# First norm and projections of a two-layer trunk: squares, scaling, partial sums and the values' first copy in another order

## The chip, the cores and the metric

The kernel runs on one NeuronCore of one Trainium2 chip. The core has five engines with an instruction queue each: TensorE (PE in the profile; its weight loads are PEld), VectorE (DVE), ScalarE (ACT), GpSimd (POOL) and SyncE (SP), which issues the transfers from memory. An engine runs its queue in order and waits, at the head of the queue, on semaphores that other engines or transfers raise. The metric is device microseconds (us) of one execution; lower is better.

## The reference

`x` is one sequence of 1024 tokens by 1024 features, `c` one vector of 1024 features. There are two layers. Layer 0 mixes tokens with softmax attention that has a forget gate (16 heads of 64), layer 1 with gated linear attention (4 heads); each is followed by a SwiGLU of 2816 hidden features. What matters here is the start of layer 0:

```python
mod = silu(c) @ ada_w[0] + ada_b[0]            # six vectors of 1024
sh1, sc1, g1, sh2, sc2, g2 = split(mod, 6)
h = rms_norm(x, norm1_g[0]) * (1 + sc1) + sh1   # norm: mean of squares over the 1024 features of a token
q, k, v, f_logit = split(h @ fox_w_in[0])       # 1024 + 1024 + 1024 + 16 columns
log_f = log_sigmoid(f_logit + b_f)
cum = cumsum(log_f, axis=tokens)
logits = q @ k.T / 8 + cum[t] - cum[s]          # causal, then softmax, times v, times fox_w_out
```

All is float32. Products are made from pairs: a tensor is split into a high part (rounded to the matmul's format fp32r) and a low part (the rest), and a product takes three matmuls, high by high, high by low, low by high.

## The kernel before

The start of the kernel (up to about 105 us) computes `h`, transposed (features on partitions), and with it, block by block, the first projections. It goes through these steps.

**Loads.** SP loads token tiles `xt[0..7]` of 128 tokens by 1024 features, the columns of `ada_w` for `sh1` and `sc1` in four pieces `d2 = 0..3` (piece `d2` gives the two vectors on the 256 features of blocks 2·d2 and 2·d2+1; tiles `adas`, two `k` of 128 rows in each), and the weights of the forget gate (`fw`), of the first two query heads (`wq0`) and key heads (`wk0`).

**Norm.** `sq_tile(t)` squares a token tile and sums over the features into `ssx` (ACT with an accumulator, L490, or DVE, L488). `ss_root(hf)` makes `1/sqrt` of four tiles' sums (DVE L494, POOL L495). `scale_tile` multiplies a tile by it in place (even tiles on DVE, L500; tiles 1 and 5 on ACT, L502; tiles 3 and 7 on POOL, L504).

**Modulation vectors.** For a piece `d2`, eight row blocks `k` are multiplied by `silu(c)` and added up. `ada0_pe` lets PE do some row blocks as matmuls with one moving column (L517, tile `mp`), `ada0_dve` lets DVE accumulate the others into `acc` (L527 the first, L529 the next ones), and `ada0_sum` adds `acc` over the partitions with four one-column matmuls (L535) and makes the two columns that `h_mod` needs (L538, L381). A one-column float32 matmul shows as two records in the profile.

**Blocks.** A block is (d, hf): feature block d of 128, token half hf of 512. `h_tr` transposes four token tiles into one PSUM bank (PE L551, tile `xp`, one bank for all blocks), `h_mod` applies the vectors (ACT L556 to `y`, ACT L558 the high part `h0h`, DVE for even d or POOL for odd d L559 the low part `h0l`), `first_k` runs the eight matmuls of the block for gate, query and key (PE L570 to L576): five need `h0h`, the last three need `h0l`. On PE a block's transposes are issued ahead of the previous block's eight matmuls.

**After the blocks.** `first_z(hf, acc)` makes the gate's logits (ACT L250, DVE L251, ACT L859, DVE L860) and, at the second half, log-sigmoid and the running sum over tokens: ACT Exp and Ln (L862, L863, each with a table load), DVE L864, the scan L865, and the transfers of the sum out and back (L866, L881). `q_evac` and `k_evac` copy the first queries and keys out of PSUM. `v_half` projects values for four heads: four token pairs `tp`, 48 matmuls each into one of two PSUM banks in turn (`vps`, L268 to L270), and `v_split` copies each pair out in two steps of ACT (L174) and DVE (L175). Then the attention loop begins; its first matmul is at L1006.

The order of the instructions of each engine from `begin` to the end of `v_half` is the order in which the program writes them: `in_order` chains them. Behind that, a planner with its own estimates places instructions.

Of the kernel before, what the change touches and what calls it, by code (L numbers as in the profile page):

```python
# [9 lines left out]
F32 = mybir.dt.float32  # L10
# [6 lines left out]
P = 128  # L17
# [36 lines left out]
def trunk(ctx, tc, x, c, ada_w, ada_b, norm1_g, norm2_g, ffn_w_in, ffn_w_out,  # L54
# [448 lines left out]
        else:  # L503
            nc.gpsimd.tensor_scalar(xs_, xs_, r, 1.0, op0=ALU.mult, op1=ALU.mult)  # L504

    NPE = (4, 0, 0, 0)
    modp = {}

    def ada0_pe(d2):

        mp = mp0([P, 2, 2], F32, f"mp{d2}")
        modp[d2] = (mp, acc2())
        n = 0
        for k in range(NPE[d2]):
            for j in range(2):
                for i in range(2):
                    nc.tensor.matmul(mp[:, j, i:i + 1], araw[(d2, k // 2)][:, k % 2, j, psl(i)], cact[:, k:k + 1],  # L517
                                     start=n == 0, stop=False)
                    n += 1

    def ada0_dve(d2, *ks):

        acc = modp[d2][1]
        for k in ks:
            a = araw[(d2, k // 2)][:, k % 2]
            if k == NPE[d2]:
                nc.vector.tensor_scalar(acc, a, cact[:, k:k + 1], None, op0=ALU.mult)  # L527
            else:
                nc.vector.scalar_tensor_tensor(acc, a, cact[:, k:k + 1], acc, op0=ALU.mult, op1=ALU.add)  # L529

    def ada0_sum(d2):
        mp, acc = modp.pop(d2)
        for j in range(2):
            for i in range(2):
                nc.tensor.matmul(mp[:, j, i:i + 1], acc[:, j, psl(i)], ones,  # L535
                                 start=NPE[d2] == 0 and j == i == 0, stop=j == 1 and i == 1)
# [318 lines left out]
    def first_z(hf, acc):  # L855
        cs = hsl(hf)
        f = zt[:, cs]
        sum16(f, ze[:, cs], acc[0][1])
        nc.scalar.activation(ze[:, cs], f, AF.Abs, bias=bf)  # L859
        nc.vector.tensor_scalar(zt[:, cs], f, bf, 0.0, op0=ALU.add, op1=ALU.min)  # L860
        if hf:
            nc.scalar.activation(ze, ze, AF.Exp, scale=-1.0)  # L862
            nc.scalar.activation(ze, ze, AF.Ln, bias=1.0)  # L863
            nc.vector.tensor_sub(zt, zt, ze)  # L864
            nc.vector.tensor_tensor_scan(cum, zt, zt, 0.0, ALU.add, ALU.bypass)  # L865
            nc.sync.dma_start(cum_d, cum)  # L866
            load_cum(0)
            load_cum(1)

    def v_split(g, tp, ps):  # L870
        v = vring([P, 2, 4, 2, 64], FR, f"v{g}{tp}")
# [21 lines left out]
    ada0_sum(0)  # L893
    wf_()
    wq0_()
    ada0_pe(1)
    ada0_dve(1, 0)
    wk0_()
    load_ada0(2)
# [4 lines left out]
    h_mod(0, 0)  # L904
    ada0_dve(1, 1, 2, 3)
    h_block(1, 0)
    ada0_dve(1, 4, 5, 6, 7)
    first_k(0, 0, accs[0])
    first_k(1, 0, accs[0])
    sq_tile(4)  # L910
    h_tr(2, 0)
    ada0_sum(1)
    sq_tile(5, True)
    h_mod(2, 0)
    h_block(3, 0)
    sq_tile(6, True)
    sq_tile(7)
    first_k(2, 0, accs[0])
    first_k(3, 0, accs[0])
    ada0_pe(2)  # L920
    ada0_dve(2, 0, 1)
    ss_root(1)
    for cs in (slice(0, HALF), slice(HALF, D)):
        for t in range(4, 8):
            scale_tile(t, cs)
    h_block(0, 1)
    ada0_dve(2, 2, 3, 4, 5, 6, 7)
    rest0 = [(0, 1), (1, 1), (2, 1), (3, 1), (4, 0), (5, 0), (4, 1), (6, 0), (7, 0), (5, 1), (6, 1), (7, 1)]
    done = []
    for n, (d, hf) in enumerate(rest0):  # L930
        if n:
            h_tr(d, hf)
        if n == 4:
            ada0_sum(2)
            ada0_pe(3)
            ada0_dve(3, 0, 1)
        if n == 7:
            ada0_sum(3)
        if n:
            h_mod(d, hf)  # L940
        if n in (4, 5, 6):
            ada0_dve(3, 2 * n - 6, 2 * n - 5)
        if n == 8:
            feed.depth = 1
            wvs[0] = [feed.next()]
        if n == 10:
            wvs[0].append(feed.next())
            first_z(0, accs[0])
        if n == 11:
            q_evac(accs[0][1][1], qkt[0], 0)  # L950
        if n:
            first_k(*rest0[n - 1], accs[rest0[n - 1][1]])
    k_evac(accs[0][2][1], qkt[0], 0)
    first_k(*rest0[-1], accs[1])
    first_z(1, accs[1])

    def v_half(g, half):

        if g not in vts:
            vts[g] = []  # L960
        if g not in wvs:
            wvs[g] = [feed.next(), feed.next()]
        for tp in range(2 * half, 2 * half + 2):
            ps = pj([P, 2, 256], F32, f"vps{g}{tp}")
            for i in range(2):
                yield from proj_tok(ps[:, i, :], wvs[g], hT, 2 * tp + i)
            v_split(g, tp, ps)
        if g or half:
            del wvs[g]

# [125 lines left out]
    acc0 = acc_r([P, 2, HALF], F32, "acc0")[:, 0, 0:256]  # L1096
    for j in (2, 3, 4, 5):
        ada0.q.append(ada_steps(0, j, acc0, wr, 4, 0))
    run(v_half(0, 0))
    q_evac(accs[1][1][1], qkt[0], 1)  # L1100
    k_evac(accs[1][2][1], qkt[0], 1)
    split_after.update((e, last_of(e)) for e in "ADG")
# [884 lines left out]
```

## Time and profile before

| | us |
|---|---|
| median of three runs (2415.0 to 2418.0) | 2417.4 |
| the profiled execution's own time | 2420.17 |
| its span | 2418.5 |
| PE busy in the span | 2369.3 |
| DVE, ACT, POOL busy | 1769.9, 1132.9, 1023.5 |
| start of the first value matmul (L268) | 79.10 |
| start of the first attention matmul (L1006) | 104.46 |

The profile is of one execution. A row of the timeline has its start, its length, engine, line, operation and tile, and in brackets how long the engine had stood idle before it and what ended that. Lengths of neighbouring matmuls overlap, so their speed is read from the distance of their starts. The table of stages gives the busy time of each engine, the clock granted to PE (1.00 is full) and the transfers' share.

### The profile page before, as it was taken

The page shows a single profiled execution, that of the slowest core. Times are in us where ns is not written, and L with a number is a line of the kernel's source. Part 1 is how long each engine was busy: PE and PEld are TensorE (multiplying, and loading weights), DVE is VectorE, ACT ScalarE, POOL GpSimd, SP SyncE. Part 2 cuts the span into 40 slices and gives each one's busy share as a digit, 9 for nine tenths or more (in the row PEclk, how much of TensorE's full clock was granted, in tenths as well). Part 3 has the DMA queues.
Part 4 walks back from the last instruction along what each step waited for, and adds up shares of the span by engine and source line. Part 5 has one row for each costly group of instructions (what it writes and reads, how often), then busy time and mean ns, then how long its engine had stood idle before and what let it go on. Part 6 is the DMA issues. An engine that isn't in the chain of part 4 may idle for free.

```text
span 2418.5 us, 35795 instructions
## 1 busy us (share of the span) xinstructions
PE 2369.3 (98%) x12328; PEld 2014.2 (83%) x12328; DVE 1769.9 (73%) x3020; ACT 1132.9 (47%) x2183; POOL 1023.5 (42%) x920
## 2 busy tenths in 40 slices
PE   6999999999999999999999999999999999999998
PEld 5888888878888888888888898888888888888888
DVE  6477878876688888876788676666587767666787
ACT  4665565666543333345324555454343334345325
POOL 3333333333335656653363222122335656653362
PEclk9999999999999999999999999999999999999999
DMA  8223423323326545457665243334325434347664
GB/s 254 63 88 96 129 82 121 115 96 114 122 90 194 178 161 173 163 184 260 226 211 170 59 127 95 114 117 167 109 92 179 157 132 156 130 169 257 230 211 148
DMA packets 340766, 359.24 MB, mean 149 GB/s; under 512 B 24220, under 2 KB 285496, under 8 KB 340584
## 3 DMA queue, kind: packets, MB, share of 16 engines
q1 hardware_dynamic: 340584, 356.95, 44.9%
q8 instruction: 97, 1.59, 0.3%
q14 instruction: 85, 0.70, 0.1%
HBM read 268.19 MB, written 88.67 MB: 148 GB/s over the span
## 4 chain that ended last, share of the span: by engine, by line
PE 85%; DVE 6%; DMA 3%; ACT 2%; issue 2%; SPq 1%; POOL 0%; DVEq 0%; POOLq 0%; ACTq 0%
PE p_b L268 16%; PE p_b L269 16%; PE p_b L270 16%; PE t_b L1038 2%; PE o_b L1052 2%; PE qk_b L268 2%; PE qk_b L269 2%; PE qk_b L270 2%; DMA ad_s<-in_ada_w_dram 1%; PE s_b L1006 1%; PE s_b L1007 1%; SPq L399 1%; PE vps_b L268 1%; PE vps_b L270 1%; PE vps_b L269 1%
## 5 line engine op out<-in xcount | busy, mean ns | idle before, releaser
L174 ACT CAST o_s<-xv_s 128x512 fp32r<-128x512 f32 (+1 forms) x376 | 217.7, 587 | 317.9 <-PE p_b L270 260.9
L175 DVE TENSOR_TENSOR o_s<-xv_s,o_s 128x512 fp32r<-128x512 f32 (+1 forms) x376 | 320.0, 854 | 59.6 <-ACT o_s L174 59.1
L269 PE MATMUL p_b<-B,o_s 128*128 128x512 f32 x608 | 237.6, 391 | 0.0
L270 PE MATMUL p_b<-B,o_s 128*128 128x512 f32 x608 | 237.0, 390 | 0.0
L268 PE MATMUL p_b<-B,o_s 128*128 128x512 f32 x608 | 236.3, 391 | 0.0
L1018 POOL TENSOR_SCALAR lp_s<-lp_s,st 128x128 f32<-128x128 f32 (+7 forms) x128 | 98.9, 777 | 288.3 <-DVE st L1017 257.5
L762 POOL TENSOR_TENSOR ex_s<-xv_s,xv_s 128x512 f32<-128x512 f32 (+1 forms) x64 | 87.7, 1371 | 271.2 <-DMA xv_s<-in_ffn_w_in_dram 107.0
L268 PE MATMUL p_b<-T,o_s 128*128 128x512 f32 x480 | 186.7, 389 | 0.0
L269 PE MATMUL p_b<-T,o_s 128*128 128x512 f32 x480 | 186.7, 389 | 0.0
L270 PE MATMUL p_b<-T,o_s 128*128 128x512 f32 x480 | 181.1, 389 | 0.0
L270 PEld LDWEIGHTS p_b<-B,o_s 128*128 128x128 f32 x608 | 114.7, 189 | 23.9
L269 PEld LDWEIGHTS p_b<-B,o_s 128*128 128x128 f32 x608 | 114.7, 189 | 23.7
L268 PEld LDWEIGHTS p_b<-B,o_s 128*128 128x128 f32 x608 | 114.7, 189 | 23.7
L1016 ACT ACTIVATE lp_s<-lp_s,st 128x128 f32<-128x128 f32 (+7 forms) x128 | 99.3, 777 | 71.4 <-DVE st L1012 69.1
L764 POOL TENSOR_TENSOR xv_s<-ex_s,xv_s 128x512 f32<-128x512 f32 (+1 forms) x64 | 84.9, 1326 | 68.8 <-DVE o_s L175 66.6
L174 ACT CAST pt_s<-t_b 128x512 fp32r<-128x512 f32 (+1 forms) x160 | 80.1, 547 | 69.1 <-PE t_b L1038 68.0
L1397 DVE TENSOR_TENSOR ex_s<-ex_s,p_b 128x512 f32<-128x512 f32 x140 | 93.7, 681 | 24.0 <-PE p_b L270 23.9
L227 POOL TENSOR_TENSOR w_l_s<-w__s,w_h_s 128x256 fp32r<-128x256 f32 x90 | 70.3, 810 | 93.9 <-ACT w_h_s L223 62.1
L175 DVE TENSOR_TENSOR pt_s<-t_b,pt_s 128x512 fp32r<-128x512 f32 (+1 forms) x160 | 96.4, 631 | 13.0 <-ACT pt_s L174 12.5
L268 PEld LDWEIGHTS p_b<-T,o_s 128*128 128x128 f32 x480 | 90.1, 188 | 18.7
L269 PEld LDWEIGHTS p_b<-T,o_s 128*128 128x128 f32 x480 | 90.1, 188 | 18.7
L270 PEld LDWEIGHTS p_b<-T,o_s 128*128 128x128 f32 x480 | 90.1, 188 | 18.6
(1937 smaller groups left out, 7404.6 us busy)
## 6 DMA issues: line engine op xcount, KB each, us to landing
xv_s<-in_ffn_w_in_dram SPq DMA_DIRECT2D x176, 256.0 KB, 3.2
hid_B<-x SPq DMA_DIRECT2D x70, 512.0 KB, 2.6
ad_s<-in_ada_w_dram SPq DMA_DIRECT2D x384, 64.0 KB, 2.4
hid_T<-x SPq DMA_DIRECT2D x36, 512.0 KB, 2.8
xv_s<-in_ffn_w_out_dram SPq DMA_DIRECT2D x96, 192.0 KB, 5.0
ada_s<-in_ada_w_dram SPq DMA_DIRECT2D x128, 128.0 KB, 2.9
xv_s<-in_ffn_w_out_dram SPq DMA_DIRECT2D x40, 256.0 KB, 2.9
T2o<-hid_T SPq DMA_DIRECT2D x18, 512.0 KB, 8.4
```

What stands on the lines that cost most here:

```text
L174: nc.scalar.copy(hi, src)
L175: nc.vector.tensor_sub(lo, src, hi.bitcast(F32))
L227: (nc.gpsimd if i < 3 else nc.vector).tensor_sub(lo[:, cs], rw[:, cs], hi[:, cs].bitcast(F32))
L268: nc.tensor.matmul(ps, ah, bh, start=start, stop=False)
L269: nc.tensor.matmul(ps, ah, bl, start=False, stop=False)
L270: nc.tensor.matmul(ps, al, bh, start=False, stop=stop)
L762: nc.gpsimd.tensor_add(s1, a21, a22)
L764: nc.gpsimd.tensor_sub(a11, s1, a11)
L1016: nc.scalar.activation(lp, lp, AF.Exp, bias=mcur, scale=-1.0, accum_out=st[:, qi, 2:3])
L1018: nc.gpsimd.tensor_scalar(lp, lp, st[:, qi, 3:4], 1.0, op0=ALU.mult, op1=ALU.mult)
L1038: nc.tensor.transpose(tp[:, i, :], lps[qi][:, psl(2 * b + jj)], ident)
L1397: nc.vector.tensor_add(d, d if src is None else dest(G, src), ps)
```

## The change

Seven edits, all in the steps above; the arithmetic is the same.

- Piece 1's row blocks 6 and 7 go from DVE to PE: `ada0_pe(1)` now issues eight one-column matmuls (sixteen records), behind the matmuls of block (1, 0).
- The squares of tiles 5 and 6 go from DVE to ACT, that of tile 7 from ACT to DVE. `ss_root(1)` is issued ahead of block (3, 0).
- The second token half's scaling is issued in two parts: features 0 to 511 ahead of block (0, 1), features 512 to 1023 (`slice(HALF, D)`) in block (4, 0)'s turn, behind two accumulation steps of piece 3.
- Piece 2's accumulation is spread differently, piece 3's starts two turns sooner, and its sum (`ada0_sum(3)`) is made a turn later, since block (5, 1) now stands ahead of (6, 0) and (7, 0).
- The value weights are split in turns 6 and 8 in place of 8 and 10.
- The first gate half (`first_z(0)`) is issued in turn 11, and the queries' copy behind the turns: both now behind the last block's `h_mod`.
- `gates_end` takes Ln, subtraction, scan and the sum's transfers out of `first_z`; `v_half` calls it behind the copy of its first token pair.

The order of SP's transfers stays the same. Far behind, at the start of layer 1 (near 1330 us), the planner also places a few instructions differently: the four matmuls that spread the norm (L601) stand nine value matmuls sooner, a value copy (ACT, DVE), a gate copy on ACT and two gate matmuls are shifted by one or two places.

```diff
-    NPE = (4, 0, 0, 0)
-    modp = {}
+
+    PE_K = (range(0, 4), range(6, 8), (), ())
+    accs0, mps0 = {}, {}
...
-        for k in range(NPE[d2]):
+        for k in PE_K[d2]:
...
         if hf:
             nc.scalar.activation(ze, ze, AF.Exp, scale=-1.0)
-            nc.scalar.activation(ze, ze, AF.Ln, bias=1.0)
-            nc.vector.tensor_sub(zt, zt, ze)
-            nc.vector.tensor_tensor_scan(cum, zt, zt, 0.0, ALU.add, ALU.bypass)
-            nc.sync.dma_start(cum_d, cum)
-            load_cum(0)
-            load_cum(1)
+
+    def gates_end():
+        nc.scalar.activation(ze, ze, AF.Ln, bias=1.0)
+        nc.vector.tensor_sub(zt, zt, ze)
+        nc.vector.tensor_tensor_scan(cum, zt, zt, 0.0, ALU.add, ALU.bypass)
+        nc.sync.dma_start(cum_d, cum)
+        load_cum(0)
+        load_cum(1)
...
-    ada0_pe(1)
     ada0_dve(1, 0)
...
     h_block(1, 0)
-    ada0_dve(1, 4, 5, 6, 7)
+    ada0_dve(1, 4, 5)
     first_k(0, 0, accs[0])
     first_k(1, 0, accs[0])
+    ada0_pe(1)
     sq_tile(4)
     h_tr(2, 0)
     ada0_sum(1)
-    sq_tile(5, True)
+    sq_tile(5)
+    sq_tile(6)
+    sq_tile(7, True)
     h_mod(2, 0)
+    ss_root(1)
     h_block(3, 0)
-    sq_tile(6, True)
-    sq_tile(7)
+    ada0_dve(2, 0)
     first_k(2, 0, accs[0])
     first_k(3, 0, accs[0])
-    ada0_pe(2)
-    ada0_dve(2, 0, 1)
-    ss_root(1)
-    for cs in (slice(0, HALF), slice(HALF, D)):
-        for t in range(4, 8):
-            scale_tile(t, cs)
+    for t in range(4, 8):
+        scale_tile(t, slice(0, HALF))
+    ada0_dve(2, 1, 2)
     h_block(0, 1)
-    ada0_dve(2, 2, 3, 4, 5, 6, 7)
-    rest0 = [(0, 1), (1, 1), (2, 1), (3, 1), (4, 0), (5, 0), (4, 1), (6, 0), (7, 0), (5, 1), (6, 1), (7, 1)]
-    done = []
+    ada0_dve(2, 3, 4, 5, 6, 7)
+    rest0 = [(0, 1), (1, 1), (2, 1), (3, 1), (4, 0), (5, 0), (4, 1), (5, 1), (6, 0), (7, 0), (6, 1), (7, 1)]
+
+    steps = {2: (0, 1), 4: (2, 3), 5: (4, 5), 6: (6, 7)}
     for n, (d, hf) in enumerate(rest0):
         if n:
             h_tr(d, hf)
         if n == 4:
             ada0_sum(2)
-            ada0_pe(3)
-            ada0_dve(3, 0, 1)
-        if n == 7:
+        if n == 8:
             ada0_sum(3)
         if n:
             h_mod(d, hf)
-        if n in (4, 5, 6):
-            ada0_dve(3, 2 * n - 6, 2 * n - 5)
-        if n == 8:
+        ada0_dve(3, *steps.get(n, ()))
+        if n == 4:
+            for t in range(4, 8):
+                scale_tile(t, slice(HALF, D))
+        if n == 6:
             feed.depth = 1
             wvs[0] = [feed.next()]
-        if n == 10:
+        if n == 8:
             wvs[0].append(feed.next())
+        if n == 11:
             first_z(0, accs[0])
-        if n == 11:
-            q_evac(accs[0][1][1], qkt[0], 0)
         if n:
             first_k(*rest0[n - 1], accs[rest0[n - 1][1]])
+    q_evac(accs[0][1][1], qkt[0], 0)
     k_evac(accs[0][2][1], qkt[0], 0)
...
-    def v_half(g, half):
+    def v_half(g, half, then=None):
...
             v_split(g, tp, ps)
+            if then is not None and tp % 2 == 0:
+                then()
...
-    run(v_half(0, 0))
+    run(v_half(0, 0, gates_end))
```

More of the change, by code (lines that the diff above doesn't have):

```diff
@@ L504, in scale_tile @@
             nc.gpsimd.tensor_scalar(xs_, xs_, r, 1.0, op0=ALU.mult, op1=ALU.mult)
-    NPE = (4, 0, 0, 0)
-    modp = {}
+    PE_K = (range(0, 4), range(6, 8), (), ())
+    accs0, mps0 = {}, {}
     def ada0_pe(d2):
-        mp = mp0([P, 2, 2], F32, f"mp{d2}")
-        modp[d2] = (mp, acc2())
+        mp = mps0[d2] = mp0([P, 2, 2], F32, f"mp{d2}")
         n = 0
-        for k in range(NPE[d2]):
+        for k in PE_K[d2]:
             for j in range(2):
@@ L521, in ada0_dve @@
     def ada0_dve(d2, *ks):
-        acc = modp[d2][1]
         for k in ks:
             a = araw[(d2, k // 2)][:, k % 2]
-            if k == NPE[d2]:
+            if d2 not in accs0:
+                acc = accs0[d2] = acc2()
                 nc.vector.tensor_scalar(acc, a, cact[:, k:k + 1], None, op0=ALU.mult)
             else:
+                acc = accs0[d2]
                 nc.vector.scalar_tensor_tensor(acc, a, cact[:, k:k + 1], acc, op0=ALU.mult, op1=ALU.add)
     def ada0_sum(d2):
-        mp, acc = modp.pop(d2)
+        if d2 not in mps0:
+            ada0_pe(d2)
+        mp, acc = mps0.pop(d2), accs0[d2]
         for j in range(2):
@@ L535, in ada0_sum @@
                 nc.tensor.matmul(mp[:, j, i:i + 1], acc[:, j, psl(i)], ones,
-                                 start=NPE[d2] == 0 and j == i == 0, stop=j == 1 and i == 1)
+                                 start=not PE_K[d2] and j == i == 0, stop=j == 1 and i == 1)
         ds_ = slice(2 * d2, 2 * d2 + 2)
```

## The prediction, made before the changed kernel had run

> **What bounds the kernel now.** The page's first part has PE busy for 98% of the span, so a gain must be PE time that is idle or slow. The table of stages shows where: up to 100 us PE is at 7 to 9 of 10, behind that at 10. I read PE's timeline there, its waits, then the engines that ended them.
>
> ```profile
> PE 2369.3 (98%) x12328; PEld 2014.2 (83%) x12328; DVE 1769.9 (73%) x3020; ACT 1132.9 (47%) x2183; POOL 1023.5 (42%) x920
> ```
> ```profile
> 30.00:40.00 10.00, 6.84 (x28) 5.40 (x28) 7.36 (x13) 3.94 (x6) 2.20 (x2) 0.83 1.08 353
> 60.00:70.00 10.00, 8.77 (x39) 7.37 (x40) 2.73 (x6) 5.04 (x8) 2.19 (x3) 0.83 0.01 2
> ```
> ```profile
> 31.84 1.05 PE L535 MATMUL mp_b<-ones,acc_s 128*128 128x1 f32 x8 [1.84 <-DVE acc_s L529]
> 34.22 0.80 PE L551 MATMUL xp_b<-ident,xt_s 128*128 128x128 f32 x4 [1.32 <-ACT y_s L556]
> 36.31 0.63 PE L572 MATMUL ks_b<-h0h,wk0h_s 128*128 128x512 f32 x1
> 36.74 0.63 PE L573 MATMUL ks_b<-h0h,wk0l_s 128*128 128x512 f32 x1
> 38.49 0.40 PE L572 MATMUL qs_b<-h0h,wq0h_s 128*128 128x512 f32 x1
> 38.72 0.39 PE L573 MATMUL qs_b<-h0h,wq0l_s 128*128 128x512 f32 x1
> ...
> 50.31 0.50 PE L574 MATMUL fs_b<-h0l,fw_s 128*128 128x512 f32 x1 [0.82 <-DVE h0l L559]
> 61.23 1.28 PE L535 MATMUL mp_b<-ones,acc_s 128*128 128x1 f32 x8 [1.75 <-DVE acc_s L529]
> 72.66 0.50 PE L574 MATMUL fs_b<-h0l,fw_s 128*128 128x512 f32 x1 [0.67 <-POOL h0l L559]
> 76.92 0.50 PE L570 MATMUL fs_b<-h0h,fw_s 128*128 128x512 f32 x1 [1.01 <-ACT h0h L558]
> ```
> ```profile
> 92.88 0.36 PE L268 MATMUL vps_b<-wv_0h_s,h0h 128*128 128x256 f32 x1 [2.13 <-DVE v_s L175]
> ```
>
> The brackets, with 0.46, 0.28 and 0.87 us more between 40 and 43, add up to 11.2 us of idle PE from 29 us on. PE also falls to half speed twice: starts of 512-column matmuls lie 0.43 us apart at 36.31 and 0.23 at 38.49. The clock of 0.83 in two stages says 1.7 us lost in each. So about 14.5 us are there to be won, 0.6% of the time.
>
> Two more rows set what DVE and POOL can do side by side:
>
> ```profile
> 36.60 1.53 DVE L527 TENSOR_SCALAR acc_s<-adas_s,cact 128x512 f32<-128x512 f32 x1
> ```
> ```profile
> 36.56 1.28 POOL L559 TENSOR_TENSOR h0l<-y_s,h0h 128x512 fp32r<-128x512 f32 x1 [9.26 <-ACT h0h L558]
> ```
>
> The same L527 takes 0.48 us alone (52.82). Here it ends 0.29 us behind POOL's instruction: a DVE instruction that starts under a POOL subtraction is held until that ends.
>
> **The change part by part,** placed on each engine in its new order, with lengths from this trace.
>
> *Piece 1's sum.* DVE loses two accumulation steps of 0.76 us: `acc` is ready at 30.2 in place of 31.8. PE gains sixteen one-column records behind 29.40. L535's records are 0.10 us apart when PE is at speed (51.6) and 0.21 when not (L517, 28 in 6.1 us): 1.6 or 3.4 us. PE had just run 512-column matmuls 0.23 apart, so I take 1.6. Transposes (0.4) follow, the sum from 31.5 (0.8), the columns (0.45), and `y` of (2, 0) starts at 32.8, not 33.38. With 3.4 us and slow transposes it starts near 35.4, and this stage ends 2.3 us later than I say.
>
> *Squares.* ACT does tiles 4, 5, 6 (1.2 us each with the accumulator's read). SP's rows that reuse a tile's semaphore put the landings of 5, 6, 7 at 29.7, 31.0, 32.3, so ACT is done at 32.3, ahead of `y`: the two added squares are hidden by the wait for piece 1, with 0.5 us to spare; a piece 1 that came sooner would gain nothing. DVE does tile 7 from 32.75 to 34.0 (1.3). Queued behind it are `h0l` of (2, 0), which PE needs only at 36.4, and L494, at 35.1. POOL's root (1.03) now stands ahead of `h0l` of (3, 0), which is then ready at 37.7; PE wants it at 38.9. Scaled halves are ready at 38.5. Before, squares, root and scaling ended at 41.5 and PE stood waiting.
>
> *PE through this stage.* Matmuls of (2, 0) start at 34.3 (before 34.87), are slow until 37.6 as before, (3, 0) ends at 39.6. Transposes, `y` 0.8, transposes: (0, 1) starts 1.5 us behind its `y`, at 41.6. Before: 43.48. **-1.9.** Behind that a block costs 2.29 us (45.44 to 47.73). DVE has five accumulation steps ahead of `h0l` of (2, 1), not six: PE waits 0.25, not 0.82. Block (3, 1) starts at 49.65 against 52.36, **-2.7** so far.
>
> *Second halves of the scaling.* They stand on DVE behind `h0l` of (4, 0) (ends 52.4) and two steps (53.9). POOL starts `h0l` of (5, 0) at about 53.95, 1.3 us. One or both of DVE's scalings (0.47 each) are held: tile 6 is ready at 55.6 to 56.0, but 54.85 if DVE gets in first. PE wants tiles 4 to 7 for block (4, 1) at 53.9. A new wait, 0.6 to 2.1 us; I take 1.9, by the 36.60 row. ACT's scaling (0.7) is ahead of that, POOL's has been done since 50. Block (5, 0) starts at 56.15 against 56.95: **-0.8** is left.
>
> *Blocks (5, 1) to (7, 1).* Piece 3's last steps run beside the three POOL subtractions of the value weights. Three DVE instructions beside such a run took 2.75 us at 22.8, so `acc` is ready at 60.5; PE comes to it at 60.75, having done (4, 1) first. The wait of 1.75 goes, and with it the slow PE behind it (1.7). The last blocks' `h_mod` no longer stand behind the gate's ACT and DVE steps (1.01). POOL's subtractions of the second value weights still delay `h0l` of (7, 0): 0.4 stays of 0.67. Transposes and the sum at speed give 0.8 more. Values start at 72.8 against 79.10: **-6.3.** SP's queue has no new order; its next weight loads wait on these subtractions and are issued earlier too.
>
> *Gate and values.* From the gate's first copy to Exp's end took 12.3 us with 1.4 of `h_mod` in it: now from 70.4 to 81.3. The first pair's copies take 1.7, so their bank is free at 83.0; PE wants it for pair 2 at 72.8 + 11.6 = 84.4. The wait of 2.13 goes, since Ln and the scan no longer stand ahead. They stand ahead of the second pair instead: table 1.28, Ln 1.07, subtraction 1.2, scan 2.3, the last copies: 89.6, wanted at 90.2. A margin of 0.6 only; without it up to 2.1 come back. The sum's transfers go out at 88.5 and took 1.9 and 3 us; the first score needs them near 98. Attention starts at 72.8 + 4 x 5.81 = 96.05 against 104.46: **-8.4.**
>
> *What is not handed on.* ACT's second-half copies start at 89.2 against 93.37, only 4.2 sooner. Pair 2's bank, free 7.3 us behind that start before, comes free at 96.5; the next projection wants it at 96.3. With the last copy DVE's first score comes 7.4 sooner. I give back 0.9, with none and 4.2 kept as ends: **-7.5.**
>
> *Layer 1.* The spread of the norm comes 1.07 us sooner (nine matmuls of 0.12), the copies that PE waited 0.91 for (1340.46) one place later on DVE (0.7): between 0.5 won and 1.3 lost (two ACT steps). I take nothing: the two cancel.
>
> The profiled execution took 2420.17, 2.8 over the median; 2412.7 in its terms, **2409.9** in the median's.
>
> **The rivals.**
>
> *The clock falls at the new wait.* The wait at 61.23 was 1.75 us and PE came out slow, losing 1.7. The new one at 54 is 1.9: the sum would be -5.8, 2411.6. Against it, the longer wait of 2.13 at 92.88 came out at speed (starts 0.12 apart), with dense matmuls on both sides, as here; ahead of 61.23 there was a sum of one-column matmuls. [...] I keep the row with dense work around it.
>
> *ACT sets the attention's start.* The page leaves ACT 40 to 60% idle there, but its list between the gate's copies and the second queries is serial. If scores follow it, 4.2 us are won: 2413.2, within the bound. For it: the margin of pair 2's bank is used up. Against: the first attention matmuls need nothing later than 96.5.
>
> *The values' wait only moves to the fourth pair.* Then 2.1 come back: -5.4, 2412.0. The margin is 0.6 us.
>
> *PE stays slow.* Between 29.4 and 34.3 PE now does one-column matmuls and transposes, and its later waits sit closer together. Each further stretch of 3.4 us at half speed costs 1.7. With five of them the gain is gone, with eight (37.6 to 65) the kernel is 6.1 us slower: 2423.5. Against it, the waits of 0.87 and 0.28 within 41 to 44 left PE at speed.
>
> **How the numbers follow.** About 0.2% (4.8 us) is what a measurement of this kernel tells from no change; the bound lies at 2412.6. Forecast 0.45, clock at the new wait 0.15, fourth pair 0.08, ACT (or another engine taking back as much) 0.23, PE slow 0.09. Faster: 0.45 + 0.15 + half of 0.08 = 0.64. Same: 0.23 + 0.04 = 0.27. Slower: 0.09. The best ends (no hold at the scaling 1.3, nothing given back 0.9, layer 1 0.5) give -10.2, 2407.2; the worst together (slow partial sum 2.3, clock 1.7, fourth pair 2.1, layer 1 1.3) leave about nothing: 2417.4. I go 1.7 below the best end, for the run's own scatter of 3 us. Without the slow-PE case and the very ends that is 8 in 10: 2405.5 to 2417.
>
> **What would show it.** Right: sixteen L517 records behind 29.4 within 1.7 us; (0, 1) at 41.6; a PE wait of about 1.9 on DVE's L500 near 54; no wait on `acc` near 60; the clock at 1.00 in 60 to 70; values at 72.8 and no PE wait on `v_s`; L1006 (now L1013) at 96. Wrong: a slow partial sum, more than one stage under 1.00, or an L1006 8 us sooner with a span that is not.

## The result, and the profile after

| | before | after |
|---|---|---|
| median of 20 runs each, us | 2419.16 | 2414.86 |
| lowest to highest | 2415.0 to 2426.69 | 2410.38 to 2418.2 |
| the profiled execution's own time | 2420.17 | 2412.18 |
| its span | 2418.5 | 2410.4 |
| first value matmul | 79.10 | 74.60 |
| first attention matmul | 104.46 | 97.66 |

The ratio is 0.9974, with a 95% interval of 0.9967 to 0.9982: of the 2417.4 us taken as the time before, 6.3 us less (4.4 to 8.0). The forecast was 7.5 less. Before attention 6.8 us are won in the two profiles.

The page's first part of the changed kernel, PE's row: PE is busy for 2.6 us less, though it has 16 records more. The other 5.5 us of the shorter span were idle.

```profile
PE 2366.7 (98%) x12344; PEld 2012.5 (83%) x12344; DVE 1771.3 (73%) x3016; ACT 1132.1 (47%) x2185; POOL 1025.0 (43%) x920
```

The table of stages of the changed kernel, four stages from 30 us on, and behind it the stage from 50 to 60 us of the kernel before (PE's busy time is the first column behind the length, the granted clock the one behind POOL):

```profile
30.00:40.00 10.00, 8.68 (x47) 7.30 (x47) 6.21 (x12) 5.81 (x9) 3.30 (x3) 0.83 1.08 355
40.00:50.00 10.00, 9.09 (x51) 6.99 (x49) 8.21 (x10) 5.60 (x8) 2.92 (x2) 1.00 0.90 276
50.00:60.00 10.00, 8.42 (x46) 6.70 (x45) 7.78 (x12) 6.07 (x10) 3.20 (x5) 1.00 0.01 2
60.00:70.00 10.00, 9.64 (x49) 7.22 (x48) 5.28 (x8) 6.12 (x10) 7.25 (x7) 1.00 0.24 65
```
```profile
50.00:60.00 10.00, 9.16 (x51) 7.55 (x51) 7.18 (x12) 4.21 (x6) 2.69 (x2) 1.00 0.00 0
```

Between 30 and 40 us PE is busy for 8.68 us, before for 6.84. From 60 to 70 the clock is 1.00, before 0.83. From 50 to 60 the stage has lost, 8.42 against 9.16: there lies the new wait.

PE's timeline of the changed kernel up to the values (its lines lie one to seven further down: L551 is L554, L535 L538, L570 L573, L574 L577, L559 L562, L529 L530, L1006 L1013):

```profile
29.76 1.84 PE L517 MATMUL mp_b<-cact,adas_s 128*128 128x1 f32 x16
31.46 0.64 PE L554 MATMUL xp_b<-ident,xt_s 128*128 128x128 f32 x4
31.94 0.95 PE L538 MATMUL mp_b<-ones,acc_s 128*128 128x1 f32 x8
34.21 0.66 PE L554 MATMUL xp_b<-ident,xt_s 128*128 128x128 f32 x4 [1.32 <-ACT y_s L559]
...
41.69 0.66 PE L554 MATMUL xp_b<-ident,xt_s 128*128 128x128 f32 x4 [0.87 <-ACT y_s L559]
42.34 0.50 PE L573 MATMUL fs_b<-h0h,fw_s 128*128 128x512 f32 x1
...
56.43 0.74 PE L554 MATMUL xp_b<-ident,xt_s 128*128 128x128 f32 x4 [1.58 <-DVE xt_s L500]
...
61.73 1.05 PE L538 MATMUL mp_b<-ones,acc_s 128*128 128x1 f32 x8
...
69.44 0.50 PE L577 MATMUL fs_b<-h0l,fw_s 128*128 128x512 f32 x1 [0.36 <-POOL h0l L562]
...
74.60 0.28 PE L268 MATMUL vps_b<-wv_0h_s,h0h 128*128 128x256 f32 x1
```

Read from the top: the sixteen L517 records of piece 1 take 1.84 us, 0.11 apart, at a granted clock of 1.00. The sum follows at 31.94; before, PE stood idle for 1.84 us ahead of it and ran it at 31.84. PE is now nearly as late as DVE was, in an execution in which block (1, 0) ended 0.36 us later (29.76 against 29.40). Transposes and `y` still cost waits of 1.32 and 0.87. Block (0, 1) starts at 42.34. At 56.43 there is the new wait of 1.58 on the second half of the scaling (L500). The sum of piece 3 at 61.73 has no bracket, so its wait of 1.75 is gone. One short wait on POOL has a bracket, and the values start at 74.60.

PE's timeline where attention begins, in the same profile:

```profile
97.66 0.22 PE L1013 MATMUL s_b<-KA,QA 128*128 128x128 f32 x1
...
98.54 0.47 PE L268 MATMUL qk_b<-h0h,w_h_s 128*128 128x512 f32 x1 [0.47 <-DVE v_s L175]
```

No value matmul waits on `v_s` any more. What is left is a wait of 0.47 at the next projection.

DVE and then POOL of the changed kernel around the new wait:

```profile
54.80 1.88 DVE L500 TENSOR_SCALAR xt_s<-xt_s,rstd 128x512 f32<-128x512 f32 x2
...
59.29 2.39 DVE L530 SCALAR_TENSOR_TENSOR acc_s<-adas_s,cact,acc_s 128x512 f32<-128x512 f32 x2
```
```profile
54.73 1.27 POOL L562 TENSOR_TENSOR h0l<-y_s,h0h 128x512 fp32r<-128x512 f32 x1 [3.56 <-ACT h0h L561]
59.24 3.02 POOL L227 TENSOR_TENSOR wv_0l_s<-wv_s,wv_0h_s 128x256 fp32r<-128x256 f32 x3 [3.24 <-ACT wv_0h_s L223]
```

DVE's two scalings start 0.07 us behind POOL's subtraction and take 1.88 us: 0.68 beyond its end at 56.00. That is the hold that the prediction read at 36.60. The pair ends only behind POOL's instruction; the 0.68 behind it is less than the 0.88 that the pair takes clear of it (the run with the scaling first, below). Up to 70 us the two traces, of before and of after, have 15 DVE instructions on 512 columns that start under a POOL subtraction, and all end 0.28 to 0.62 us behind it. For DVE instructions of every kind, as the prediction has it, the rows do not show a hold: L541 and L251 of the changed kernel, which read `mp_b` and `fs_b`, start at 62.82 and 73.00 and end at 62.98 and 73.68, while POOL's L562 runs from 62.22 to 63.68 and from 72.45 to 73.74.

### The profile page after: what moved, and what is told of

It is laid out like the page before. It is cut to its first block, busy times and chain, and to the rows that moved or that the text cites. A ratio compares the mean times of both kernels' runs of the same rounds, so it can differ in the third digit from the quotient of the medians.

```text
span 2410.4 us, 35830 instructions
## 1 busy us (share of the span) xinstructions
PE 2366.7 (98%) x12344; PEld 2012.5 (83%) x12344; DVE 1771.3 (73%) x3016; ACT 1132.1 (47%) x2185; POOL 1025.0 (43%) x920
## 4 chain that ended last, share of the span: by engine, by line
PE 81%; DVE 8%; DMA 5%; ACT 2%; issue 2%; SPq 1%; POOL 1%; DVEq 0%; POOLq 0%; ACTq 0%
PE p_b L270 16%; PE p_b L268 16%; PE p_b L269 16%; PE o_b L1059 2%; PE t_b L1045 2%; PE qk_b L268 1%; PE qk_b L269 1%; PE qk_b L270 1%; DMA adas_s<-in_ada_w_dram 1%; PE s_b L1013 1%; PE s_b L1014 1%; PE vps_b L268 1%; PE vps_b L270 1%; PE vps_b L269 1%; DMA ad_s<-in_ada_w_dram 1%
## 5 line engine op out<-in xcount | busy, mean ns | idle before, releaser
L175 DVE TENSOR_TENSOR o_s<-xv_s,o_s 128x512 fp32r<-128x512 f32 (+1 forms) x376 | 322.5, 861 | 58.5 <-ACT o_s L174 57.6
```

Of the source, the lines that this page charges most:

```text
L175: nc.vector.tensor_sub(lo, src, hi.bitcast(F32))
```

## The experiments

Executions differ by up to 2.2 us already where their PE does the same, since the loads land at different times: DVE's first step of piece 1 (L527) starts, when a transfer has ended its wait, at 22.46 in "gates ahead" and at 23.91 in "DVE sooner", the runs with the first and the last mark. A mark helps: the end of the matmuls of block (1, 0) on PE, ahead of the edits' first effect on PE. It lies at 29.40 before and at 29.76 after. Column "from mark" is the distance from there to the first attention matmul. It serves among the runs built on the changed kernel, where PE's own records lead from the mark to the sum of piece 1. In the kernel before and in "gates alone" that sum waits for DVE and starts at 31.84 and 31.86, though their marks lie 0.51 us apart; those two are compared by their rows.

Times of the three groups of runs were taken beside 31, 17 and 21 runs of the kernel before (medians 2420.5, 2422.57, 2420.14).

| run | mark | values | attention | from mark | median us (runs) | ratio to before |
|---|---|---|---|---|---|---|
| before | 29.40 | 79.10 | 104.46 | 75.06 | | |
| after | 29.76 | 74.60 | 97.66 | 67.90 | 2414.86 (20) | 0.9974 (0.9967 to 0.9982) |
| gates ahead | 28.48 | 73.59 | see text | | 2418.83 (10) | 0.9995 (0.9986 to 1.0004) |
| gates alone | 29.91 | 79.09 | 102.12 | 72.21 | 2417.77 (10) | 0.9992 (0.9980 to 1.0003) |
| scaling first | 30.04 | 77.73 | 100.80 | 70.76 | 2415.57 (10) | 0.9981 (0.9971 to 0.9990) |
| squares back | 29.58 | 74.97 | 98.05 | 68.47 | 2414.69 (10) | 0.9978 (0.9968 to 0.9987) |
| DVE sooner | 30.63 | 73.74 | 96.79 | 66.16 | 2412.93 (6) | 0.9964 (0.9952 to 0.9976) |
| one block on PE | 29.54 | 73.82 | 96.90 | 67.36 | 2416.51 (1) | |
| filled gap | 29.93 | 73.82 | 96.91 | 66.98 | 2411.76 (1) | |
| PE delayed | 30.52 | 75.31 | 105.31 | 74.79 | 2416.52 (11) | 0.9976 (0.9966 to 0.9987) |
| delayed twice | 28.79 | 73.37 | 110.32 | 81.53 | 2427.74 (11) | 1.0027 (1.0018 to 1.0036) |
| after again | 29.59 | 74.29 | 97.36 | 67.77 | 2413.64 (9) | 0.9978 (0.9968 to 0.9988) |
| three together | 30.28 | 72.10 | 95.17 | 64.89 | 2413.95 (7) | 0.9968 (0.9954 to 0.9982) |

### The gates ahead of the values' first copy again

```diff
-    run(v_half(0, 0, gates_end))
+    gates_end()
+    run(v_half(0, 0))
```

> The changed kernel with one part undone: Ln, subtraction, scan and the sum's transfers stand ahead of the values' first copy again. In the changed kernel Exp ends at 83.3 and the values start at 74.6; pair 3 wants the first bank at 86.2. With Ln (2.35), subtraction (1.2) and scan (2.3) ahead, DVE's first copy starts at 89.3 and the bank is free near 90.5. Theory (the edit pays what the copies' place costs): PE waits about 4.3 us on v_s at the third pair, the first attention matmul moves from 97.7 to 101.5, the time rises by about 4. Rival (the edit is worth the 2.1 us of wait that the kernel before showed): first attention matmul near 99.8, time up by 2.

PE's wait at the values' third pair and the clock around it, in this run:

```profile
89.58 0.36 PE L268 MATMUL vps_b<-wv_0h_s,h0h 128*128 128x256 f32 x1 [3.70 <-DVE v_s L175]
```
```profile
87.60:91.00 3.40, 1.42 (x12) 1.45 (x13) 2.16 (x5) 1.83 (x5) 0.00 (x0) 1.00 0.12 19
91.00:94.40 3.40, 3.40 (x19) 3.40 (x18) 2.08 (x4) 3.34 (x7) 0.10 (x1) 0.50 0.92 277
```

The values start at 73.59, and PE then waits 3.70 us for `v_s`, where the changed kernel does not wait. The second line of the clock's table adds what had not been priced: behind the wait PE runs at half speed for 3.4 us, which is another 1.7. The planner put the first score matmuls into the gap (85.11), so the next projection is compared in place of them: 102.65, from the mark 74.17, against 98.54 and 68.78 after. That is 5.4 us later, more than the theory (about 4) and the rival (2) had, and the time's ratio is 0.9995 in place of 0.9974, which is 5.1 us, plus or minus 2.8. So this one edit carries most of the gain, but only on top of the others: the earlier PE comes to the values, the longer it would wait for the gate.

### The gates' edit alone, on the kernel before

```diff
-            nc.scalar.activation(ze, ze, AF.Ln, bias=1.0)
...
-    run(v_half(0, 0))
+    run(v_half(0, 0, gates_end))
```

> The kernel before with this one part alone: the values' first copy between Exp and Ln. Theory: the wait of 2.13 us at the third pair goes and no wait takes its place (second pair's bank free at 93.9, wanted at 96.5); first attention matmul at 102.3 in place of 104.46, time 2 us less. Rival: the wait moves to the fourth pair, first attention matmul stays at 104.4 and so does the time.

The first attention matmul of this run, on PE's timeline:

```profile
102.12 0.22 PE L1010 MATMUL s_b<-KA,QA 128*128 128x128 f32 x1
```

And the sum of piece 1, which waits for DVE as it does before:

```profile
31.86 1.05 PE L535 MATMUL mp_b<-ones,acc_s 128*128 128x1 f32 x8 [1.35 <-DVE acc_s L529]
```

Attention comes 2.3 us sooner than before, and no value matmul waits: the bracket of 2.13 at 92.88 went, and nothing took its place. (The distance from the mark shrinks by 2.85. The 0.5 more is no gain: the mark came 0.51 later here, and PE then waited 1.35 for DVE, not 1.84.) The time's ratio of 0.9992 has an interval that holds 1; a gain of this size does not show in 10 runs. With the run above: 2.3 us alone, 5.4 with the others. The two groups of edits are not additive.

### The scaling ahead of the two accumulation steps

```diff
+        if n == 4:
+            for t in range(4, 8):
+                scale_tile(t, slice(HALF, D))
         ada0_dve(3, *steps.get(n, ()))
-        if n == 4:
-            for t in range(4, 8):
-                scale_tile(t, slice(HALF, D))
```

> The changed kernel with the second halves' scaling ahead of piece 3's two accumulation steps on DVE. Theory (DVE's sum of work up to piece 3's sum is the limit there, and scaling is held by POOL's subtraction): both scalings take 0.95 us in place of 1.88 as no POOL subtraction runs beside them; PE's wait of 1.58 us on the scaled tile goes; but piece 3's accumulation still ends near 61, so PE waits 1.0 to 1.5 us on acc there and the first attention matmul gains 0.5 or less (97.2 to 97.7). Rival (the wait is the whole cost): first attention matmul at 96.1, time 1.6 us less.

DVE's scalings, PE's waits and the stage from 60 to 70 us of this run:

```profile
53.63 0.88 DVE L500 TENSOR_SCALAR xt_s<-xt_s,rstd 128x512 f32<-128x512 f32 x2
```
```profile
60.12 0.50 PE L577 MATMUL fs_b<-h0l,fw_s 128*128 128x512 f32 x1 [1.09 <-DVE h0l L562]
...
62.93 1.87 PE L538 MATMUL mp_b<-ones,acc_s 128*128 128x1 f32 x8 [1.41 <-DVE acc_s L530]
```
```profile
60.00:70.00 10.00, 8.47 (x31) 7.00 (x32) 4.73 (x8) 3.06 (x5) 4.62 (x5) 0.66 0.17 52
```

Clear of POOL's subtraction the two scalings take 0.88 us in place of 1.88, and PE does not wait for them. But the accumulation steps now stand where the scalings stood, `acc` and a low part are late, and PE waits 1.09 and 1.41. In the changed kernel one wait of 1.58 had cost 1.58; here two within 3 us bring two stretches at half speed (0.66 in the table) on top. Attention starts 2.9 us later from the mark, worse than either theory had it. The wait at 56.43 is not to be had by this move alone: DVE is behind with its list between 52 and 62 us, and what is put ahead makes something else late.

### DVE's accumulation sooner as well

```diff
-    ada0_dve(2, 1, 2)
+    ada0_dve(2, 1, 2, 3, 4)
     h_block(0, 1)
-    ada0_dve(2, 3, 4, 5, 6, 7)
-    steps = {2: (0, 1), 4: (2, 3), 5: (4, 5), 6: (6, 7)}
+    ada0_dve(2, 5, 6, 7)
+    steps = {2: (0, 1), 3: (2, 3), 4: (4,), 5: (5,), 6: (6, 7)}
```

with the scaling first, as in the run before.

> The changed kernel with the second halves' scaling first, and with DVE's accumulation steps moved up into DVE's own idle time: piece 2's steps 3 and 4 ahead of block (0, 1) (DVE stood idle there for 1.6 us), piece 3's steps 2 and 3 a turn sooner. Theory (both PE's wait at block (4, 1) and piece 3's sum are DVE's work being late): no wait on the scaled tile, piece 3's sum at 59.9 in place of 61.7, values start at 72.7, first attention matmul at 95.8, time about 2 us less than the changed kernel. Rival (POOL's subtractions or ACT's list set the pace behind 55 us): the wait goes, but the first attention matmul stays within 0.6 of 97.7.

PE's transposes of the block that waited for the scaling, and the sum of piece 3, in this run:

```profile
55.70 0.60 PE L554 MATMUL xp_b<-ident,xt_s 128*128 128x128 f32 x4
...
60.86 1.05 PE L538 MATMUL mp_b<-ones,acc_s 128*128 128x1 f32 x8
```

Both waits are gone, and nothing is late behind them. Attention starts 1.7 us sooner than after, from the mark: the 1.58 and a little more. The median is the lowest of the kernels with several runs, 2412.93; the ratio of 0.9964 and that of after, 0.9974, overlap in their intervals, so a gain in time over the changed kernel is likely and not shown.

### The squares back on their engines

```diff
-    sq_tile(5)
-    sq_tile(6)
-    sq_tile(7, True)
+    sq_tile(5, True)
     h_mod(2, 0)
-    ss_root(1)
     h_block(3, 0)
-    ada0_dve(2, 0)
+    sq_tile(6, True)
+    sq_tile(7)
     first_k(2, 0, accs[0])
     first_k(3, 0, accs[0])
+    ada0_dve(2, 0)
+    ss_root(1)
```

> The changed kernel with the squares undone: tiles 5 and 6 squared on DVE, tile 7 on ACT, in the places of before, and the root behind block (3, 0). Theory (by rows: L494 near 38.0, root until 39.2, tile 6 scaled at 40.5, while PE comes free at 40.2): block (0, 1) starts 0.3 to 1.2 us later than 42.34, the first attention matmul moves by as much, the time by about 0.5. Rival (the squares' new engines pay the whole 1.9 us that the prediction gives to this stage): (0, 1) near 44.2, first attention matmul near 99.5.

Attention starts 0.6 us later from the mark; the ratio is 0.9978. So the squares' engines hardly matter once DVE is rid of two accumulation steps: what had made PE stand in 40 to 43 before was the sum of all that DVE had to do there. That last step is read from DVE's list; no run takes its other parts out one by one.

### One row block of piece 1 on PE in place of two

```diff
-    PE_K = (range(0, 4), range(6, 8), (), ())
+    PE_K = (range(0, 4), range(7, 8), (), ())
...
-    ada0_dve(1, 4, 5)
+    ada0_dve(1, 4, 5, 6)
```

> The changed kernel with one row block of piece 1 on PE in place of two (DVE does six). In the changed kernel PE's sixteen records took 1.84 us and piece 1's sum came no sooner than before (y at 33.38 in both). Theory (PE is now the later of the two): eight records take 0.9, DVE ends at 31.3, the sum starts at 31.3, y at 32.8, block (0, 1) 0.3 to 0.5 us sooner. Rival (DVE is the later): y at 33.4 or later, nothing gained.

The eight records take 0.95 us, and attention starts 0.5 us sooner from the mark (one execution). Two blocks on PE were one too many: with one, DVE and PE are ready at nearly the same time.

### The gap behind piece 1's sum, filled

```diff
     ada0_sum(1)
+    for _ in range(5):
+        nc.tensor.matmul(accs[1][0][1], wf[:, 0, :], hT[0].hi[:, hsl(0)], start=True, stop=True)
```

These five matmuls are added work; a later one overwrites their result.

> The changed kernel with five added matmuls of 512 columns, written to a bank that is not yet in use, behind piece 1's sum, where PE waits 1.3 us for y. They add work without use. Theory (the half speed from 34.2 to 37.6 comes from too little work in the 3.4 us ahead of it): the matmuls of (2, 0) run 0.23 us apart, not 0.43, block (3, 0) ends near 38.4 in place of 40.2, PE waits for the scaled tiles until about 39.0, and the first attention matmul moves by -1.0 to -1.2. Rival (the clock does not answer to such a filling, or the one-column matmuls ahead of it have already set it): (2, 0) still runs 0.43 us apart, the rest moves by 0 to +0.3.

PE's timeline in the gap, and the stage from 30 to 40 us, in this run:

```profile
32.91 1.41 PE L919 MATMUL fs_b<-h0h,fw_s 128*128 128x512 f32 x5
34.38 0.66 PE L554 MATMUL xp_b<-ident,xt_s 128*128 128x128 f32 x4
```
```profile
30.00:40.00 10.00, 9.81 (x58) 7.50 (x56) 5.67 (x11) 5.54 (x10) 3.31 (x3) 1.00 1.08 353
```

The five take 1.41 us where PE had waited 1.32. The clock of the stage is 1.00 in place of 0.83, and attention starts 0.9 us sooner from the mark. Of the 1.7 us that the half speed had cost, 1.2 have arrived at the end of block (3, 0) (39.18 here, 40.22 after, with the marks taken off) and 1.05 at the start of (0, 1), 41.46 here; the rest goes in gaps too short for brackets, where PE is now ahead of what it needs: the low part's matmul at 38.38 starts 0.46 behind the one before (its neighbours 0.23), and the transposes at 39.18 take 0.76 (0.60 after). The theory had 1.0 to 1.2. That half speed here goes with too little work on PE is shown: in the 3.4 us from 31.60 PE is busy for 3.34 here and for 2.08 after; the eleven profiles without these matmuls all have a stretch that begins between 33 and 36 us in which a 512-column matmul takes 0.63 us, the two with them (this one and the last run below) have none, their 512-column matmuls there take 0.39 to 0.50.

### TensorE delayed, by 7 and by 14 us

```diff
+            if (g, tp) == (0, 2):
+                for _ in range(58):
+                    nc.tensor.matmul(ps[:, 0, :], hT[0].hi[:, psl(0)], wvs[0][0].hi[:, 0, :], start=True, stop=True)
```

These are added work too; the second run has 116 of them.

> The changed kernel with 58 added matmuls of 256 columns (0.12 us each, 7.0 us, results overwritten) ahead of the third token pair: PE comes to attention as late as in the kernel before, all the rest is as changed. Theory (what PE gains at the start is handed on to the end): first attention matmul at 104.2 to 104.7, time equal to the kernel before within its scatter, ratio 1.000 (0.999 to 1.001). Rival (a later stage takes such shifts back, or the planner's other order in layer 1 has its own part): the time stays 2 us or more below the kernel before.

> The changed kernel with 116 matmuls of 256 columns, whose result is overwritten, ahead of the third token pair of the values: twice the 58 of the run before, about 14 us of TensorE alone. They are added work; the rest is computed in full. Attention's first score matmul should come near 112.3 us (105.31 with 58, 97.7 without). Theory A (time lost by TensorE ahead of attention is handed on, and the loss that did not show with 58 was scatter of the later stages): the last score matmul near 572.6 + 14 = 587, the time near 2429. Theory B (the other engines use such a delay to get ahead, a fixed amount of about 3 us, and the rest is handed on): last score near 584, time near 2426. Theory C (TensorE follows another engine through most of the layer, so that delays of this size are nearly all absorbed): last score under 581, time under 2421.

The score matmuls (first form only) of the changed kernel, of the run with 58 and of the run with 116: the last two numbers before the semicolon are the first and the last start.

```profile
L1013 PE MATMUL s_b<-KA,QA x96: 220/387/522, 97.7 to 572.6; 128*128 128x512 f32 x40, 128*128 128x256 f32 x24, 128*128 128x384 f32 x24, 128*128 128x128 f32 x8
```
```profile
L1016 PE MATMUL s_b<-KA,QA x96: 220/386/497, 105.3 to 576.7; 128*128 128x512 f32 x40, 128*128 128x256 f32 x24, 128*128 128x384 f32 x24, 128*128 128x128 f32 x8
```
```profile
L1016 PE MATMUL s_b<-KA,QA x96: 220/387/522, 110.3 to 582.9; 128*128 128x512 f32 x40, 128*128 128x256 f32 x24, 128*128 128x384 f32 x24, 128*128 128x128 f32 x8
```

From the mark the first score comes 6.9 and 13.6 us later than after, the last one 3.3 and 11.3. Attention takes 3.6 and 2.3 back. Of the 3.6, 1.7 are a stretch at half speed at 355.9 us that after has and the run with 58 has not (clock of 0.91 and of 1.00 from 350 to 370); 1.9 and 2.3 are what is left. PE's waits between 85 and 650 us add up to 9.6 us in after, 8.3 and 8.1 in these two, so most of that is waits that disappear. So the other engines do get ahead by about 2 us, and the rest is handed on as far as there. With 116 that is theory B (584 at the last score; measured 582.9, or 583.9 at the mark of after); the median time of 2427.74 lies between B's 2426 and A's 2429.

In time, 116 matmuls cost 11.9 us by the ratios (1.0027 against 0.9978, plus or minus 3.3), which agrees with the 11.3 that were left at the last score. The 58 cost only 0.5 (0.9976 against 0.9974, plus or minus 3.1). By the terms set for it that run went the rival's way: PE comes to attention 0.9 us later than in the kernel before, and the time stays 5.9 us under that kernel's.

The granted clocks on record say where these 5.9 us are. Their mean is 0.9932 in the 17 runs of the kernel before and 0.9956 in the eleven with 58. The time lost at half speed, estimated as (1 - clock) times the time, is 16.4 and 10.5 us, so by this estimate the whole difference of the two means is less half speed (4.1 to 4.8 of it by the slopes of time on clock given further down), and at an equal clock the run with 58 takes about the time of the kernel before, as the theory has it. One stretch less is traced, the one near 62 us (1.7). The rest lies, by the profiles, behind attention's start, where neither theory nor rival had looked; why half speed comes less often there stays open.

### The changed kernel again, and three edits together

> The changed kernel as it is, once more, timed on the same chip and beside the same runs of the kernel before as the two others. If the earlier comparison holds: 0.9974 of before, 2414 to 2415.5 us, and attention's first matmul within 1 us of 97.7. It also gives a second profile, in which the half-speed stretches behind 300 us should lie elsewhere or be others in number, if they are scatter of the execution and no property of the kernel.

The score matmuls of this second profile:

```profile
L1013 PE MATMUL s_b<-KA,QA x96: 220/388/499, 97.4 to 572.5; 128*128 128x512 f32 x40, 128*128 128x256 f32 x24, 128*128 128x384 f32 x24, 128*128 128x128 f32 x8
```

Its first and last score lie within 0.3 us of the first profile's, and the ratio is 0.9978. The stretches at half speed behind 300 us lie in the stages 350 to 370, 660 to 680 and 1310 to 1330 us (clock of 0.91 in each), in the first in 350 to 370, 1310 to 1330 and 1750 to 1770 (again 0.91 each): which of them come differs between executions of one kernel. Each costs up to 1.7 us, so one or two more or fewer move a profile by as much as half of this change. The timed runs scatter with them: time and granted clock correlate at -0.75 over the 20 runs of the changed kernel, at -0.77 over the 69 of the kernel before. Their mean number is not the same in the two kernels, though: the clock is 0.9950 and 0.9952 in the two sets of the changed kernel, 0.9934 in the 69.

The three edits (DVE sooner with the scaling first, one row block on PE, the filled gap) in one kernel:

> Three edits on the changed kernel together: the accumulation steps of DVE placed sooner and the scaling of the second halves ahead of them; one row block of piece 1's sum on TensorE in place of two (eight records, DVE does the other); five 512-column matmuls with a result that is overwritten in TensorE's gap behind that sum. Alone, with the start of the run taken off, they brought attention's first matmul 1.8, 0.5 and 0.9 us forward. If they add up: 94.5 (97.7 in the changed kernel), no half-speed stretch between 30 and 45 us, no wait on the scaled tiles, and a time of 2411.5, 3 us under the changed kernel on the same chip. Rival: ScalarE's list from the gate's copies to the second queries sets the attention's start by then, so that the second and third edit add nothing: 96, 2413.

Piece 1's records on PE and the stage from 30 to 40 us of this run:

```profile
30.28 0.95 PE L517 MATMUL mp_b<-cact,adas_s 128*128 128x1 f32 x8
31.08 0.63 PE L554 MATMUL xp_b<-ident,xt_s 128*128 128x128 f32 x4
```
```profile
30.00:40.00 10.00, 9.34 (x51) 6.90 (x50) 7.50 (x13) 6.71 (x12) 3.31 (x3) 1.00 1.08 354
```

Full clock, no wait on the scaled tiles, and 3.0 us sooner from the mark, of 1.7 + 0.5 + 0.9 = 3.1: they add up, and ScalarE's list does not set attention's start. The time does not follow as clearly: 2413.95, ratio 0.9968 (0.9954 to 0.9982), beside 2413.64 and 0.9978 for the changed kernel in the same group. Between 650 and 1800 us the profile taken has five steps of 3.4 us at half speed against two (clock of 0.97, 0.95 and 0.97 in 650 to 700, 1300 to 1400 and 1740 to 1800, after 1.00, 0.98 and 0.97), up to 5.1 us more lost, which hides the gain in that execution. A faster kernel than the changed one is likely by the trace and not shown by the times.

## Why the prediction was right, and where its steps were off

The sign and the size of the whole were right, the size partly by luck (last step of the list). Where a step says so, the mark's 0.36 us are taken off, since the execution after came to the mark that much later than the one that the sum started from.

- **Piece 1's sum.** Right that sixteen records run 0.11 apart and not 0.21 (1.84 us, said 1.6). The sum came at 31.94, 31.58 with the mark's 0.36 off (said 31.5); `y` at 33.38, 33.02 with it off (said 32.8). By the rows nothing is won, since `y` was at 33.38 before too, but the loads were later in that execution (DVE's accumulation behind `h0l` starts at 25.70, before at 25.43); of the 0.6 that this step was to win about 0.2 is missing. The run with one row block shows what was left there, 0.5.
- **Squares.** Right that they cost nothing: undone, they lose 0.6.
- **Block (0, 1).** Said 1.9 sooner; it is 1.1 by the rows (42.34 against 43.48), 1.5 with the mark off. Of the 0.4 missing, 0.2 is that of piece 1's sum; the rest came up in PE's path from `y` to (0, 1).
- **The new wait.** Said 1.9 on L500 near 54, measured 1.58 at 56.43. Of it 1.0 is the hold by POOL's subtraction, shown by the 0.88 us of the run with the scaling first against 1.88; the rest is that DVE comes late to the scaling, shown by the run with DVE's accumulation sooner as well, where the wait goes and nothing is late behind it.
- **Blocks (5, 1) to (7, 1).** Right that the wait on `acc` and the slow clock behind it go. Mis-sized: DVE's two steps beside POOL's run of 3.02 us were done at 61.68, not 60.5, PE came to the sum at 61.73, not 60.75, and from there to the values went 12.87 us where 12.05 had been left (short waits of 0.1 to 0.36 at four blocks among them). The values start at 74.60, not 72.8: 4.5 won (4.9 with the mark off), not 6.3.
- **The gate and the values.** Right that the wait on `v_s` goes and that the fourth pair has no new one: from the values' start to attention 23.06 us, before 25.36, 2.3 won (said 2.13). Attention at 97.66 is 6.8 sooner, 7.2 with the mark off; said 8.4, and the difference is that of the steps above. What the sum did not say is how much hangs on this one edit: without it PE, sooner at the values, would have waited 3.70 and lost its clock, and 5.4 of that gain would not have arrived (first experiment).
- **What is given back.** Said 0.9, seen 0.47, on the copy of a value pair. At the last score matmul 6.0 of the 6.8 us are left (572.6 against 578.6), although after has the half-speed stretch at 355.9 and before has none in attention.
- **Layer 1.** Nothing, as said, within what half-speed stretches scatter there.
- **The time.** Said 7.5, measured 6.3. The sum prices the half speed only up to 100 us: 1.7, for the stretch near 62. By the estimate used above, the nine runs of the changed kernel lose 11.5 us to half speed, the 21 of before beside them 16.0: 4.5 (plus or minus 1.9) of the 6.4 us between their means. Within the runs of one kernel the time falls by less than that estimate has it, 1.7 us (before) and 2.0 us (changed) per 0.001 of clock, which would make it 3.1 to 3.6. So by these estimates between 1.4 and 2.8 us were won by fewer half-speed stretches later on, a term that the sum does not have. At an equal clock 2.0 to 3.4 us are left, where the steps above won about 5 at attention apart from the stretch near 62. That the two errors nearly cancel was luck; where the difference is lost is open.

Of the rivals, the clock at the new wait did not fall: 1.00 from 50 to 60. The half-speed stretch that starts at 34.6 in before lasts 3.4 us, and so do the one at 61.9 and the one at 35.0 in after. Two tables, of before and of after, each cut into steps of that length (from the start of its half-speed stretches, 3.4 us at a time):

```profile
31.20:34.60 3.40, 1.44 (x12) 1.35 (x12) 2.11 (x5) 1.18 (x2) 0.00 (x0) 1.00 1.09 350
34.60:38.00 3.40, 3.40 (x10) 2.54 (x9) 3.15 (x4) 2.76 (x5) 1.28 (x1) 0.50 1.10 349
58.50:61.90 3.40, 1.65 (x13) 1.27 (x12) 2.64 (x4) 0.16 (x1) 0.00 (x0) 1.00 0.00 0
61.90:65.30 3.40, 3.40 (x11) 2.82 (x11) 1.02 (x3) 1.40 (x2) 0.00 (x0) 0.50 0.03 7
89.20:92.60 3.40, 1.56 (x14) 1.35 (x12) 2.93 (x4) 0.65 (x2) 0.00 (x0) 1.00 0.08 12
92.60:96.00 3.40, 3.12 (x26) 3.15 (x27) 2.27 (x5) 2.84 (x6) 0.00 (x0) 1.00 0.46 119
```
```profile
31.60:35.00 3.40, 2.08 (x18) 1.76 (x17) 1.69 (x5) 2.44 (x5) 0.00 (x0) 1.00 1.09 352
35.00:38.40 3.40, 3.40 (x9) 2.63 (x10) 2.47 (x5) 2.02 (x3) 2.71 (x3) 0.50 1.09 348
52.10:55.50 3.40, 2.75 (x14) 1.92 (x13) 2.73 (x4) 2.52 (x4) 0.77 (x1) 1.00 0.01 2
55.50:58.90 3.40, 2.47 (x13) 1.98 (x14) 2.81 (x5) 1.66 (x3) 0.50 (x1) 1.00 0.00 0
```

In these two profiles every half-speed stretch between 30 and 2400 us lasts one step of 3.4 us or two (before from 34.6, 61.9, 672.9 and 1324.8, the last two for two; after from 35.0, 355.9, 1318.4 and 1755.4), and within a profile they start whole steps apart (34.6 and 61.9 before: eight steps). The step ahead of a fall need not be idle: PE was busy for 1.44, 1.65 and 2.08 us of those in the tables. The wait of 1.58 straddles two steps, so that each has 2.75 and 2.47 us of work, and the clock stays. That place was not what saved it: in "gates ahead" and in "filled gap" the same wait (1.56) lies wholly inside one step, from 53.45 and from 52.93, with 1.85 us of work in each, and the clock stays at 1.00 there too. These are dense matmuls on both sides, the reason that the prediction gave against this rival. Between 89.2 and 92.6 before, 1.56 us of dense 256-column matmuls were enough, and 1.65 with one-column matmuls among them were not (58.5), nor were 1.42 of dense matmuls (gates ahead, from 87.6). That one-column matmuls count for less is argued from these lines, not shown.

ScalarE did not set attention's start (the three edits together move it by their sum); the fourth pair did not wait; PE did not stay slow.

## What to carry to other kernels

Price a wait that an edit removes at what it would be after the other edits of the same change, not at its length in the profile of before: here 2.13 became 3.70, and the edit was worth 5.4 us with the others and 2.3 alone. Where an engine waits in the order of its list, moving one instruction forward only renames the wait if the engine is short of time there; move the whole backlog. Near a stretch with several short waits on PE, read PE's busy time in steps of 3.4 us as well: here steps with 1.42 us of work or less cost another 1.7, and so did some with up to 2.08 where one-column matmuls were among it, while 1.56 to 1.93 us of dense matmuls alone did not. And compare the granted clock of the timed runs, not only their times: a part of a gain can be half speed far behind the edits.

## What the runs showed of the hardware that was not expected

- The clock falls behind a step in which PE was busy in part: 1.40 us of 3.4 (scaling first, at 59.2), 1.42 (gates ahead, at 87.6), 1.44 and 1.65 (before), 2.08 (after). It stays with 1.56 (before, at 89.2), 1.85 (gates ahead, at 53.45, and filled gap, at 52.93) and 1.93 (squares back, at 55.04). With five added matmuls of 1.41 us in the gap it stayed at 1.00 from 30 to 40 us (0.83 after).
- A delay of PE alone by 7 or 14 us in front of attention is handed on but for about 2 us as far as the last score matmul, where every earlier loss of PE had been expected to arrive in full.
- Executions of one kernel differ in granted clock (0.991 to 0.996 over 69 runs of the kernel before), and their times with it: 1.7 to 2.0 us per 0.001.
